# Queries and keys of attention groups 2 and 3 by seven products of quarters

## The chip, the cores and the metric

The kernel runs on one core of a Trainium2 chip. The metric is the device time of one execution in microseconds (us); the time before is the median of three runs. The engines are TensorE (PE in the profile; PEld are its weight loads), VectorE (DVE), ScalarE (ACT), GpSimd (POOL) and SyncE (SP, which issues most DMAs). Each engine works through its own instructions in a fixed order, and semaphores make one engine wait for another.

## The reference

Two layers over 512 tokens of 1024 features, all in float32. Each layer is a token mixer and a gated feed-forward part, both with RMS norms, and shifts, scales and gates made from a condition vector `c` (`ada_w`). Layer 1 mixes with a recurrent mixer (HGRN2), layer 2 with dilated attention. What the change touches is the start of the attention:

```python
proj = (u @ w_in).reshape(B, S, N_GROUPS, 3, ATT_HEADS, ATT_HEAD_DIM)   # 3 groups, 8 heads of 128
for gi, (window, dilation) in enumerate(((128, 1), (512, 4), (2048, 16))):
    q = apply_partial_rope(proj[:, :, gi, 0], cos, sin) * scale
    k = apply_partial_rope(proj[:, :, gi, 1], cos, sin)
    v = proj[:, :, gi, 2]
    o_g, lse_g = dilated_group_attention(q, k, v, window, dilation)
# softmax over the groups' lse weighs the o_g; then o @ w_out
```

So queries are u (512 x 1024) times a 1024 x 128 matrix for each head and group, and keys likewise. With its transpose, one head and group gives a 256 x 1024 weight matrix (128 rows for queries, 128 for keys) times a 1024 x 512 matrix of inputs.

## The kernel before, in words

Every product in float32 precision is made of three matmuls on rounded operands: a value is cut into a rounded part `hi` and a remainder `lo` (ACT copies, then DVE subtracts), and `three` (L437 to L440) adds hi x hi, hi x lo and lo x hi into a PSUM bank. `block` (L442) does this for eight tiles of 128 input features: 24 matmuls with a 128 x 128 weight and 512 tokens.

Weights come through `Stream` (L38). It holds a list of items in the order of use; `fill` loads them into two `raw` buffers of 128 x 2048, `process_to` cuts an item into one of three `hi` and three `lo` buffers (L88 on ACT, L89 on DVE). Between attention weights, items of `ada_w` for the condition vector are woven in; they occupy `raw` buffers too, and DVE multiplies and adds them up (L257, L259), after which POOL reduces over partitions (L261).

The feed-forward parts already use Strassen's scheme in Winograd's form with seven products of quarters instead of eight (`seven_products`, L771 on, products at L853): the inputs' quarters and four sums of them (`th`, `tl`) are made once per layer by `token_sums` (L753), and for each weight block POOL (L824) and DVE (L828, L832) make the sums of weight quarters, and ACT copies partial sums from one PSUM bank into half of another (L883, L892), onto which PE goes on accumulating. There the order of instructions of all engines is written out by hand. Items of the kind "quarters" are four DMAs that lay a weight block out by its four quarters (L56 to L59). The values of groups 2 and 3 are made by seven products as well (`seven_values`, L1383).

In attention the inputs are permuted so that tokens of one residue modulo 4 lie together (`apart`, L1674, with remainders in `apart[1]`). The sums of the quarters of `apart` lie in `uh` and `ul` as `th`, `tl` (L1679 to L1681). The loop at L1852 goes over the units: for head `i` and group `g`, `st.take()` gives the weights (with two items processed ahead), `block` makes queries and then keys, and `qk_evac` (L1694) writes them from PSUM to SBUF on ACT (L1704 the 32 rotary rows, L1705 all rows). `turn_pair` (L1709) applies the rotation on DVE and copies it back on ACT. After each of the six blocks of a head `fl.tick()` runs what is due: scores (L1724), merges, transposes (L1807) and the products with the values of an earlier head. The units of head 1 in groups 1 and 2 come before the first values, then group 3 of head 1 and heads 2 to 5, then the second half of the values, then heads 6 to 8. In this part a scheduler orders each engine's instructions when the kernel is built, by its own estimates of time; it is not written out by hand.

Of the kernel before, what the change touches and what calls it, by code (L numbers as in the profile page):

```python
# [9 lines left out]
F32 = mybir.dt.float32  # L10
# [5 lines left out]
P = 128  # L16
# [21 lines left out]
class Stream:  # L38
# [73 lines left out]
    def whole(self):  # L112

        assert self.items[self.done][0] in WHOLE
        self.fill()
        self.done += 1
        return self.raw.pop(self.done - 1)
# [41 lines left out]
def block_kernel(tc, x, c, positions, ada_w, ada_b, norm_g, hgrn_w_in, lower, hgrn_norm_g, hgrn_w_out,  # L159
# [8 lines left out]
    with ExitStack() as ctx:  # L168
# [215 lines left out]

        def aqk(g, hd):
            return ("w", tuple(AW[:, (g * 3 + k) * D + hd * P:(g * 3 + k) * D + (hd + 1) * P].rearrange(
                "(k p) n -> p k n", p=P) for k in range(2)))
# [49 lines left out]
        def three(ps, ah, al, bh, bl, start, stop):  # L437
            pe.matmul(ps, ah, bh, start=start, stop=False)  # L438
            pe.matmul(ps, ah, bl, start=False, stop=False)  # L439
            pe.matmul(ps, al, bh, start=False, stop=stop)  # L440
# [942 lines left out]
        def seven_values(dsts, apart, th, tl):  # L1383
# [45 lines left out]
            def run(ps, i, tile, o, us):  # L1429
                hi, lo = tiles[i, tile]  # L1430
                for n in range(2):
                    for kt in range(4):
                        w = slice(o * 1024 + kt * 256, o * 1024 + (kt + 1) * 256)
                        three(ps[:, n * 256:(n + 1) * 256], *us(kt, n), hi[:, w], lo[:, w], kt == 0, kt == 3)
# [415 lines left out]

        fl.n = 0
        for kind, g, i in order:  # L1852
            if kind == "v":
                if g == 1:

                    for fn in fl.at.pop(fl.n, []):
                        fn()
                    seven_values(V[1:], apart, th, tl)
                    if i:
                        act.dma_start(V[0], v_away)  # L1860
                continue
            if g == 0:
                heads[i] = {}
                n = fl.n
                fl.add(n + 3, lambda i=i: scores(i, 0))
                fl.add(n + 5, lambda i=i: scores(i, 1))
                fl.add(n + 7, lambda i=i: scores(i, 2))
                fl.add(n + 9, lambda i=i: (merge_r(i), merge_n(i)))
                fl.add(n + 10, lambda i=i: flips_r(i))
                fl.add(n + 11, lambda i=i: pv_r(i))  # L1870
                fl.add(n + 11, lambda i=i: flips_n(i))
                fl.add(n + 12, lambda i=i: pv_n(i))
            whi, wlo = st.take()
            pair = []
            for k in range(2):
                ps = block(whi, wlo, k * D, P, u=apart)
                heads[i]["qk"[k], g] = qk_evac(ps, g, k, pair)
                if k == 1:
                    turn_pair(g, pair)
# [39 lines left out]
```

## Time and profile before

| | |
|---|---|
| median of 3 runs | 1510.74 us (1510.27 to 1512.08) |
| the profiled execution | 1511.44 us, its span 1509.4 us |
| granted TensorE clock, mean | 0.997 |
| DMA | 199.14 MB, mean 132 GB/s |
| ACT busy | 746.6 us (49%) |
| POOL busy | 199.0 us (13%) |

The span is the time from the first to the last instruction of the profiled execution. Busy time is the time in which an engine had at least one instruction under way. Rows that group instructions give the line, the engine, the operation, output and inputs, shapes and number, then the sum of their durations in us and the mean in ns, then the idle time before them and what ended it. In rows by time the first two columns are start and duration in us. A window row gives the stretch and its length, then the busy time and number of instructions of each engine, and at its end the granted clock, the DMA share and GB/s.

### The profile page before, as it was taken

How to read it: one execution, taken by the hardware profiler on the slowest of the kernel's cores; microseconds unless marked ns; L12 is line 12 of the kernel's file. 1: busy time of each engine (PE TensorE's matmuls, PEld its weight loads, DVE VectorE, ACT ScalarE, POOL GpSimd, SP SyncE). 2: the span in 40 equal slices, each digit the busy share in tenths (PEclk: the TensorE clock that was granted, in tenths of full speed). 3: DMA queues.
4: the chain of work that ended last, by engine and by line, in shares of the span. 5: the costliest groups of instructions: out<-in, count | busy, mean ns of one | idle time of the engine just before them, and what ended most of it. 6: DMA issues, size and time to landing. Idle time of an engine off the chain costs nothing. (4 is left out here: it accounts for less than half of the span.)

```text
span 1509.4 us, 23492 instructions
## 1 busy us (share of the span) xinstructions
PE 1493.7 (99%) x9231; PEld 1309.7 (87%) x9231; DVE 1040.2 (69%) x1807; ACT 746.6 (49%) x1321; POOL 199.0 (13%) x174
## 2 busy tenths in 40 slices
PE   8999999999999999999999999999999999999998
PEld 6777888898999988888988888988888899999886
DVE  4587768486888876577668766686466978887533
ACT  4443433362555542376546666356655555555231
POOL 1011211030111101040001110011002211110100
PEclk9999999999999999999999999999999999999999
DMA  9553444125333356424166540365213333334531
GB/s 309 166 183 126 156 152 168 56 85 167 101 109 107 107 200 213 155 108 141 57 183 191 151 120 29 123 185 141 84 52 117 100 97 112 112 112 141 199 108 56
DMA packets 206942, 199.14 MB, mean 132 GB/s; under 512 B 6840, under 2 KB 164720, under 8 KB 206576
## 3 DMA queue, kind: packets, MB, share of 16 engines
q1 hardware_dynamic: 203856, 190.87, 40.3%
q10 hardware_dynamic: 1952, 6.65, 1.2%
q8 instruction: 72, 1.18, 0.3%
q0 software_dynamic: 1024, 0.13, 0.2%
q14 instruction: 38, 0.31, 0.1%
HBM read 192.31 MB, written 5.31 MB: 131 GB/s over the span
## 5 line engine op out<-in xcount | busy, mean ns | idle before, releaser
L88 ACT CAST hi<-raw 128x2048 fp32r<-128x2048 f32 x68 | 129.7, 1907 | 199.1 <-DMA raw<-in_ffn_w_out_dram 60.8
L89 DVE TENSOR_TENSOR lo<-raw,hi 128x2048 fp32r<-128x2048 f32 x68 | 161.5, 2377 | 96.2 <-ACT hi L88 96.2
L438 PE MATMUL ps_mm<-apart,hi 128*128 128x512 f32 x384 | 151.4, 394 | 0.0
L439 PE MATMUL ps_mm<-apart,hi 128*128 128x512 f32 x384 | 151.2, 394 | 0.0
L440 PE MATMUL ps_mm<-apart,lo 128*128 128x512 f32 x384 | 150.6, 393 | 0.0
L438 PE MATMUL ps_mm<-uh,hi 128*128 128x512 f32 (+1 forms) x400 | 146.3, 366 | 0.0
L439 PE MATMUL ps_mm<-ul,hi 128*128 128x512 f32 (+1 forms) x400 | 144.3, 361 | 1.0 <-DVE ul L538 1.0
L440 PE MATMUL ps_mm<-uh,lo 128*128 128x512 f32 (+1 forms) x400 | 144.6, 361 | 0.0
L438 PE MATMUL ps_mm<-hi,oh 128*128 128x512 f32 x240 | 94.0, 392 | 0.0
L853 PE MATMUL ps_mm<-th,hiq 128*128 128x256 f32 x340 | 93.9, 276 | 0.0
L853 PE MATMUL ps_mm<-tl,hiq 128*128 128x256 f32 x340 | 93.9, 276 | 0.0
L853 PE MATMUL ps_mm<-th,loq 128*128 128x256 f32 x340 | 93.9, 276 | 0.0
L439 PE MATMUL ps_mm<-lo,oh 128*128 128x512 f32 x240 | 93.4, 389 | 0.0
L438 PEld LDWEIGHTS ps_mm<-uh,hi 128*128 128x128 f32 x400 | 75.5, 189 | 19.7 <-issue 8.4
L844 DVE TENSOR_TENSOR loq<-raw,hiq 128x1024 fp32r<-128x1024 f32 x68 | 80.2, 1221 | 16.8 <-ACT hiq L840 16.8
L439 PEld LDWEIGHTS ps_mm<-ul,hi 128*128 128x128 f32 x400 | 75.6, 189 | 12.1 <-DVE ul L538 1.4
L440 PEld LDWEIGHTS ps_mm<-uh,lo 128*128 128x128 f32 x400 | 75.5, 189 | 11.4
L824 POOL TENSOR_TENSOR raw<-raw 128x512 f32<-128x512 f32 x34 | 45.1, 1328 | 305.1 <-DVE spare L820 131.3
L440 PEld LDWEIGHTS ps_mm<-apart,lo 128*128 128x128 f32 x384 | 72.2, 188 | 14.5
L439 PEld LDWEIGHTS ps_mm<-apart,hi 128*128 128x128 f32 x384 | 72.2, 188 | 14.2
L438 PEld LDWEIGHTS ps_mm<-apart,hi 128*128 128x128 f32 x384 | 72.2, 188 | 14.1
L259 DVE SCALAR_TENSOR_TENSOR shared<-raw,cond,shared 128x512 f32<-128x512 f32 x98 | 73.2, 747 | 12.9 <-DMA raw<-in_ada_w_dram 11.9
(440 smaller groups left out, 4183.5 us busy)
## 6 DMA issues: line engine op xcount, KB each, us to landing
raw<-in_ada_w_dram SPq DMA_DIRECT2D x40, 1024.0 KB, 5.1
raw<-in_ffn_w_in_dram SPq DMA_DIRECT2D x136, 256.0 KB, 3.6
raw<-in_attn_w_in_dram SPq DMA_DIRECT2D x48, 512.0 KB, 5.1
raw<-in_ffn_w_out_dram SPq DMA_DIRECT2D x22, 1024.0 KB, 4.9
raw<-in_hgrn_w_in_dram SPq DMA_DIRECT2D x12, 1024.0 KB, 5.4
raw<-in_attn_w_in_dram SPq DMA_DIRECT2D x12, 1024.0 KB, 4.9
raw<-in_ffn_w_in_dram SPq DMA_DIRECT2D x10, 1024.0 KB, 5.0
first<-in_ada_w_dram SPq DMA_DIRECT2D x14, 512.0 KB, 7.9
```

The lines of the kernel that those rows point to most:

```text
L88: self.nc.scalar.copy(hi, t)
L89: self.nc.vector.tensor_sub(lo, t, hi.bitcast(F32))
L259: dve.scalar_tensor_tensor(a, r[:, k], sc, a, op0=OP.mult, op1=OP.add)
L438: pe.matmul(ps, ah, bh, start=start, stop=False)
L439: pe.matmul(ps, ah, bl, start=False, stop=False)
L440: pe.matmul(ps, al, bh, start=False, stop=stop)
L824: pool.tensor_add(r[:, 2], r[:, 2], r[:, 0])
L844: dve.tensor_sub(lo, src, hi.bitcast(F32))
L853: pe.matmul(ps, w[x][:, a], us[kt][y], start=begin and kt + m == 0, stop=kt == 3 and m == 2, skip_group_check=True)
```

## The change

For groups 2 and 3 (`g > 0`) of all eight heads, the items of the stream become "quarters": the four quarters of the 256 x 1024 weight matrix, of 128 x 512 each, with keys first. `sevens` makes a unit out of seven products of quarters, each of 4 x 3 matmuls with 256 tokens. `prepare_1` makes three of the seven weight operands in a first pair of hi/lo buffers: quarter 1 (its remainder on POOL), the sum of quarters 1 and 0, and that sum plus quarter 2. Quarter 0 gets quarter 2 added on POOL. `prepare_2` cuts all four places of the altered `raw` into a second pair. `products_1` makes three products, and copies partial sums on ACT from `first` to `u2` and from `u2` to `u4`; `products_2` adds the other four onto them. The queries come straight out of two banks, on ACT, with their sign turned. The keys are two sums on DVE of an SBUF copy (`xs`) and a PSUM bank. Each unit takes half of each of the four "mm" banks. Group 1 keeps its two blocks. `queries_keys` prepares up to two steps ahead of the products (a unit by seven is two steps). `three` passes `skip_group_check` on to the matmuls, and in `seven_values` only the first matmul of a bank has the start flag, where each half had it. `whole` first processes what stands ahead of it in the stream. The scheduler orders this part as before.

```diff
--- before.py
+++ after.py
@@ -111,7 +111,7 @@
 
     def whole(self):
 
-        assert self.items[self.done][0] in WHOLE
+        self.process_to(next(i for i in range(self.done, len(self.items)) if self.items[i][0] in WHOLE))
         self.fill()
         self.done += 1
         return self.raw.pop(self.done - 1)
@@ -382,9 +382,11 @@
         def av(g, hf):
             return [wtok(AW, kq, (g * 3 + 2) * D + hf * 512) for kq in range(2)]
 
+        by_seven = lambda g: g > 0
+
         def aqk(g, hd):
-            return ("w", tuple(AW[:, (g * 3 + k) * D + hd * P:(g * 3 + k) * D + (hd + 1) * P].rearrange(
-                "(k p) n -> p k n", p=P) for k in range(2)))
+            w = [AW[:, (g * 3 + k) * D + hd * P:(g * 3 + k) * D + (hd + 1) * P].rearrange("(k p) n -> p k n", p=P) for k in range(2)]
+            return ("quarters", (w[1], w[0])) if by_seven(g) else ("w", tuple(w))
 
         order, at = [], []
 
@@ -434,10 +436,10 @@
             act.copy(hi, src)
             dve.tensor_sub(lo, src, hi.bitcast(F32))
 
-        def three(ps, ah, al, bh, bl, start, stop):
-            pe.matmul(ps, ah, bh, start=start, stop=False)
-            pe.matmul(ps, ah, bl, start=False, stop=False)
-            pe.matmul(ps, al, bh, start=False, stop=stop)
+        def three(ps, ah, al, bh, bl, start, stop, part=False):
+            pe.matmul(ps, ah, bh, start=start, stop=False, skip_group_check=part)
+            pe.matmul(ps, ah, bl, start=False, stop=False, skip_group_check=part)
+            pe.matmul(ps, al, bh, start=False, stop=stop, skip_group_check=part)
 
         def block(whi, wlo, c0, width, ps=None, tok=slice(0, S), kts=range(KT), u=(uh, ul)):
 
@@ -1431,7 +1433,7 @@
                 for n in range(2):
                     for kt in range(4):
                         w = slice(o * 1024 + kt * 256, o * 1024 + (kt + 1) * 256)
-                        three(ps[:, n * 256:(n + 1) * 256], *us(kt, n), hi[:, w], lo[:, w], kt == 0, kt == 3)
+                        three(ps[:, n * 256:(n + 1) * 256], *us(kt, n), hi[:, w], lo[:, w], kt + n == 0, kt == 3, True)
 
             H2 = lambda a: a.rearrange("p (n c) -> p n c", n=2)
             for step in range(3):
@@ -1848,36 +1850,143 @@
                     pe.matmul(b[:, sl], V[0][:, t - 1, hs], st_["p0"][:, sl], start=False, stop=True)
             dve.tensor_add(oT[hd], oT[hd], b)
 
+        def sevens(g, hd):
+
+
+            raw, hi_lo = [], [None, None]
+            Q = lambda t, k, n=1: t[:, k * 512:(k + n) * 512]
+            a_of = lambda r, c: [[a[:, r * 4 + k, c * 256:c * 256 + 256] for a in apart] for k in range(4)]
+            t_of = lambda i: [[a[:, i, k] for a in (th, tl)] for k in range(4)]
+            t1, T3, T4, t2 = (t_of(i) for i in range(4))
+
+            def cut(part, k, sub):
+                hi, lo = hi_lo[0]
+                act.copy(Q(hi, part), Q(raw[0], k))
+                sub.tensor_sub(Q(lo, part), Q(raw[0], k), Q(hi, part).bitcast(F32))
+
+            def add(to, k, eng):
+                eng.tensor_add(Q(raw[0], to), Q(raw[0], to), Q(raw[0], k))
+
+            def prepare_1():
+                raw.append(st.whole())
+                hi_lo[0] = st.part_tiles(R0)
+                cut(0, 1, pool)
+                add(1, 0, dve)
+                cut(1, 1, dve)
+                add(0, 2, pool)
+                add(1, 2, dve)
+                cut(2, 1, dve)
+                add(1, 3, dve)
+
+            def prepare_2():
+                hi, lo = hi_lo[1] = st.part_tiles(R0)
+                t = raw.pop()
+                act.copy(hi, t)
+                dve.tensor_sub(lo, t, hi.bitcast(F32))
+                st.fill()
+
+            def run(ps, half, part, us, begin):
+                hi, lo = hi_lo[half]
+                for kt in range(4):
+                    w = slice(part * 512 + kt * P, part * 512 + (kt + 1) * P)
+                    three(ps, hi[:, w], lo[:, w], *us[kt], begin and kt == 0, kt == 3, True)
+
+            def products_1():
+                first, both, u2, u4 = banks = [bank("mm")[:, 0:256] for _ in range(4)]
+                xs = fresh(mk, [P, 512], "xs", 1)
+                run(first, 0, 0, a_of(0, 0), True)
+                act.copy(u2, first)
+                run(both, 0, 1, T3, True)
+                act.copy(xs[:, 0:256], both)
+                run(u2, 0, 2, t2, False)
+                act.copy(u4, u2)
+                return banks, xs
+
+            def products_2(banks, xs):
+                first, both, u2, u4 = banks
+                flip_no[1] += 1
+                o = flip_no[1] % 2 * 256
+                rows = shared[:, 1, o:o + 256]
+                q, k = (fresh(mk, [P, S], "qk", 6) for _ in range(2))
+                heads[hd]["q", g], heads[hd]["k", g] = q, k
+                lo, hi = slice(0, 256), slice(256, 512)
+                run(first, 1, 3, a_of(1, 0), False)
+                act.activation(rows[0:32], first[0:32], AF.Copy, scale=-SCALE)
+                act.activation(q[:, lo], first, AF.Copy, scale=-SCALE)
+                run(u4, 1, 0, t1, False)
+                act.copy(xs[:, 256:512], u4)
+                run(u2, 1, 2, T4, False)
+                dve.tensor_add(k[:, hi], xs[:, 256:512], both)
+                dve.tensor_add(k[:, lo], xs[:, 0:256], u2)
+                act.copy(rows[96:P], k[0:32, hi])
+                act.copy(rows[64:96], k[0:32, lo])
+                run(u4, 1, 1, a_of(1, 1), False)
+                act.activation(rows[32:64], u4[0:32], AF.Copy, scale=-SCALE)
+                act.activation(q[:, hi], u4, AF.Copy, scale=-SCALE)
+                turn_pair(g, [rows, q, k])
+            got = []
+            return [(prepare_1, lambda: got.extend(products_1())), (prepare_2, lambda: products_2(*got))]
+
+        def plain(g, hd):
+            got = []
+
+            def prepare():
+                got.extend(st.take(0))
+
+            def products():
+                pair = []
+                for k in range(2):
+                    ps = block(*got, k * D, P, u=apart)
+                    heads[hd]["qk"[k], g] = qk_evac(ps, g, k, pair)
+                    if k == 1:
+                        turn_pair(g, pair)
+                    fl.tick()
+            return [(prepare, products)]
+
+        def begin_head(i):
+            heads[i] = {}
+            n = fl.n
+            fl.add(n + 3, lambda: scores(i, 0))
+            fl.add(n + 5, lambda: scores(i, 1))
+            fl.add(n + 7, lambda: scores(i, 2))
+            fl.add(n + 9, lambda: (merge_r(i), merge_n(i)))
+            fl.add(n + 10, lambda: flips_r(i))
+            fl.add(n + 11, lambda: pv_r(i))
+            fl.add(n + 11, lambda: flips_n(i))
+            fl.add(n + 12, lambda: pv_n(i))
+
+        def queries_keys(units):
+
+            steps = []
+            for g, hd in units:
+                two = sevens(g, hd) if by_seven(g) else plain(g, hd)
+                steps += [(g, hd, k, *p) for k, p in enumerate(two)]
+            ahead = 0
+            for n, (g, hd, k, prepare, products) in enumerate(steps):
+                while ahead < min(len(steps), n + 3):
+                    steps[ahead][3]()
+                    ahead += 1
+                if (g, k) == (0, 0):
+                    begin_head(hd)
+                products()
+                if by_seven(g):
+                    fl.tick()
+
         fl.n = 0
+        units = []
         for kind, g, i in order:
-            if kind == "v":
-                if g == 1:
-
-                    for fn in fl.at.pop(fl.n, []):
-                        fn()
-                    seven_values(V[1:], apart, th, tl)
-                    if i:
-                        act.dma_start(V[0], v_away)
-                continue
-            if g == 0:
-                heads[i] = {}
-                n = fl.n
-                fl.add(n + 3, lambda i=i: scores(i, 0))
-                fl.add(n + 5, lambda i=i: scores(i, 1))
-                fl.add(n + 7, lambda i=i: scores(i, 2))
-                fl.add(n + 9, lambda i=i: (merge_r(i), merge_n(i)))
-                fl.add(n + 10, lambda i=i: flips_r(i))
-                fl.add(n + 11, lambda i=i: pv_r(i))
-                fl.add(n + 11, lambda i=i: flips_n(i))
-                fl.add(n + 12, lambda i=i: pv_n(i))
-            whi, wlo = st.take()
-            pair = []
-            for k in range(2):
-                ps = block(whi, wlo, k * D, P, u=apart)
-                heads[i]["qk"[k], g] = qk_evac(ps, g, k, pair)
-                if k == 1:
-                    turn_pair(g, pair)
-                fl.tick()
+            if kind == "qk":
+                units.append((g, i))
+            elif g == 1:
+                queries_keys(units)
+                units = []
+
+                for fn in fl.at.pop(fl.n, []):
+                    fn()
+                seven_values(V[1:], apart, th, tl)
+                if i:
+                    act.dma_start(V[0], v_away)
+        queries_keys(units)
         fl.at.clear()
         upx.close()
         tail = {-1: [lambda: pv_n(6), lambda: scores(7, 2), mkx.close], 2: [lambda: merge_r(7), back(0)], 3: [lambda: merge_n(7)],
```

## The prediction

> **What bounds the kernel now.** I read the page's engine rows first, then busy time by stage, then what PE waits for.
>
> ```profile
> PE 1493.7 (99%) x9231; PEld 1309.7 (87%) x9231; DVE 1040.2 (69%) x1807; ACT 746.6 (49%) x1321; POOL 199.0 (13%) x174
> ```
> ```profile
> 400.00:500.00 100.00, 100.00 (x878) 100.00 (x877) 80.44 (x83) 58.46 (x95) 12.93 (x10) 1.00 0.38 108
> 740.00:760.00 20.00, 20.00 (x171) 20.00 (x170) 16.12 (x20) 7.84 (x8) 0.58 (x1) 1.00 0.17 54
> 780.00:944.00 164.00, 163.63 (x834) 138.05 (x833) 114.56 (x339) 104.43 (x221) 24.16 (x20) 1.00 0.44 129
> 992.00:1120.00 128.00, 127.84 (x659) 108.68 (x658) 76.99 (x253) 82.74 (x177) 15.23 (x16) 1.00 0.40 116
> ```
> ```profile
> PE ps_b L1837 <- ACT h L1815: 0.3, 1, 0.3
> ```
>
> After the length of a stage, each window row gives PE, PEld, DVE, ACT and POOL with their counts, then the granted clock, DMA share and rate. The rows are the seven products of the first feed-forward part (400 to 500), those of the values (740 to 760), and the two stretches that make queries and keys: 780 to 944 (group 3 of head 1, heads 2 to 5) and 992 to 1120 (heads 6 to 8). In both PE does not stop; the last row is its whole list of waits from 775 to 945, 0.3 us. So these stretches last as long as PE's work, and matmul time taken out of them is won while no other engine becomes late. DVE is next: 114.6 of 164 us (70%) in the first, 77.0 of 128 (60%) in the second. The first has more because the products of the condition vector with its weights are woven into it.
>
> **PE's part.** A unit (queries and keys of one head and group) is 48 matmuls 512 wide; by seven products it is 7 x 12 = 84 matmuls 256 wide. Durations of matmuls overlap, so I count starts.
>
> ```profile
> 804.76 0.39 PE L439 MATMUL ps_mm<-apart,hi 128*128 128x512 f32 x1
> ...
> 815.19 0.39 PE L440 MATMUL ps_mm<-apart,lo 128*128 128x512 f32 x1
> ```
>
> The second is the 46th after the first: 10.43 / 46 = 0.2267 us each, 48 x 0.2267 = 10.88 us a unit. For 256 columns, the values' window has 171 in 20 us, 0.1170 each, a unit 9.82; the feed-forward window has 878 in 100 us, 0.1139 each, a unit 9.57. A unit saves 1.06 or 1.31 us, the sixteen units of groups 2 and 3 save 16.9 or 21.0. I take 16.9, since the values read the same tiles (apart, and the sums in uh and ul) through the same helper; 21.0 stays as a bound. The small matmuls of the scores are untouched.
>
> [...]
>
> **What is added for it.** Rows for the same operations elsewhere (mean ns of one after the comma):
>
> ```profile
> L832 DVE TENSOR_TENSOR raw<-raw 128x512 f32<-128x512 f32 x34 | 23.5, 691 | 1.1
> L435 DVE TENSOR_TENSOR ol<-mid,oh 128x512 fp32r<-128x512 f32 x44 | 29.8, 686 | 25.8 <-ACT oh L434 25.7
> L860 DVE TENSOR_TENSOR shared<-shared,ps_a 128x256 f32<-128x256 f32 x17 | 7.0, 413 | 0.0
> L824 POOL TENSOR_TENSOR raw<-raw 128x512 f32<-128x512 f32 x34 | 45.1, 1328 | 305.1 <-DVE spare L820 131.3 <-DVE loq L820 119.4 <-DMA raw<-in_ffn_w_in_dram 54.4
> L538 POOL TENSOR_TENSOR ul<-u,uh 128x512 fp32r<-128x512 f32 x20 | 30.4, 1545 | 7.4 <-ACT uh L534 7.4
> L434 ACT CAST oh<-mid 128x512 fp32r<-128x512 f32 x44 | 26.2, 619 | 62.3 <-PE ps_b L439 47.7 <-PE ps_mm L439 10.4 <-DVE shared L259 1.4
> L892 ACT COPY ps_mm<-ps_mm 128x256 f32<-128x256 f32 x34 | 12.1, 357 | 33.6 <-PE ps_mm L853 33.6
> L904 ACT COPY shared<-ps_mm 128x256 f32<-128x256 f32 x34 | 12.7, 372 | 4.8 <-PE ps_mm L853 4.7
> L905 ACT ACTIVATE shared<-ps_b 128x256 f32<-128x256 f32 x17 | 6.6, 390 | 0.0
> L1705 ACT ACTIVATE qk<-ps_mm 128x512 f32<-128x512 f32 x48 | 28.8, 599 | 0.9
> ```
> ```profile
> 811.30 0.68 DVE L306 TENSOR_TENSOR gate<-shared,raw 128x512 f32<-128x512 f32 x1
> 811.91 0.15 DVE L1791 TENSOR_TENSOR wE<-wE,wZ 128x4 f32<-128x4 f32 x1
> ```
>
> DVE gets, per unit, three sums and two remainders of 512 and two key sums of 256 out of PSUM: 5 x 0.69 + 2 x 0.41 = 4.27 us. The two rows in order of time show the next instruction starting 0.61 us into a 0.68 us one; the windows count that overlap once, so with 0.07 off each it is 3.8 us. ACT gets three copies of 512 (1.86), four of PSUM (2 x 0.357 + 2 x 0.372 = 1.46) and two query halves (0.78), and loses two evacuations (1.20): 2.9 us. POOL gets one remainder and one sum, 1.5 + 1.3. The 2048-wide copy and remainder stay. The 32-row copies are as many as before. DMA brings the same bytes in four pieces.
>
> ACT in the first stretch: 104.4 + 9 x 2.9 = 130.5 of about 154 us, 85%, and it is not the limit. **DVE is.** Nine units by seven lie in this stretch, six in the second, one (head 1, group 2) before the first values. First stretch: PE 164 - 9 x 1.06 = 154.5; DVE 114.6 + 9 x 3.8 = 148.8, 96%. Second: PE 128 - 6.4 = 121.6; DVE 77.0 + 22.8 = 99.8, 82%, about the 80% at which the feed-forward window runs without a stop.
>
> There is one more charge. In time order, POOL's sum and a DVE instruction with two SBUF inputs, then the same DVE instruction with POOL quiet:
>
> ```profile
> 433.84 1.29 POOL L824 TENSOR_TENSOR raw<-raw 128x512 f32<-128x512 f32 x1 [8.31 <-DVE spare L820]
> ...
> 434.47 1.21 DVE L862 SCALAR_TENSOR_TENSOR mid<-shared 128x512 f32<-128x512 f32 x1
> ```
> ```profile
> 531.94 0.68 DVE L862 SCALAR_TENSOR_TENSOR mid<-shared 128x512 f32<-128x512 f32 x1
> ```
>
> DVE, started 0.63 us after POOL, lost 0.53 us. An overlapped POOL instruction can thus cost DVE from 0 (DVE waiting for it, or working out of PSUM) to its 1.3 us. I take 0.53, as in this row: 18 such in the first stretch, 9.5 us, and 12 in the second, 6.4.
>
> So in the first stretch DVE needs 148.8 + 9.5 = 158.3 us, more than PE's 154.5. It also waits in order for ACT's copies and for scores. I put that at 3 us of those of its 49 idle us that cannot be filled (bounds 0, and 12, a quarter): 161.3 us, 2.7 saved instead of 9.5. A plain unit's weights go through one copy and one remainder, 4.3 us:
>
> ```profile
> L88 ACT CAST hi<-raw 128x2048 fp32r<-128x2048 f32 x68 | 129.7, 1907 | 199.1 <-DMA raw<-in_ffn_w_out_dram 60.8 <-PE ps_mm L439 40.0 <-DMA raw<-in_attn_w_in_dram 31.9
> L89 DVE TENSOR_TENSOR lo<-raw,hi 128x2048 fp32r<-128x2048 f32 x68 | 161.5, 2377 | 96.2 <-ACT hi L88 96.2
> ```
>
> The new chain is ACT, POOL, DVE, ACT, DVE, DVE, ACT, DVE, DVE, ACT, DVE: 3 x 0.62 + 1.55 + 5 x 0.69 + 1.91 + 2.38 = 11.2 us, and a unit now takes two of the three hi/lo buffers. Its first half can begin when the unit before the last is done, one unit (9.8 us) ahead of its use, and needs 6.2 of them. So DVE cannot work far ahead, and behind a late remainder of DVE stand PE's next product, in order, and POOL's and ACT's next steps.
>
> In the second stretch DVE has 106.2 us of 121.6; PE's gain of 6.4 holds less 1.5 where the stretch begins. Unit 2 of head 1 gains 1.1; it holds one of two raw buffers longer, and already before, the values' second half waited for its load:
>
> ```profile
> 714.66 2.00 ACT L1395 CAST hiq<-raw 128x1024 fp32r<-128x1024 f32 x2 [3.29 <-DMA raw<-in_attn_w_in_dram]
> ```
>
> I take 1.5 us lost there (bounds 0 and the chain's 11.2 - 4.3 = 6.9 us). Sum: 2.7 + 4.9 - 0.4 = 7.2 us; I take 6.5 for the profiled run of 1511.44 us (span 1509.4), which is 0.05% above the median 1510.74: **1505 us**.
>
> **Rivals.** (a) *All of it is won*: POOL's steps fall where DVE waits anyway, and the scheduler hides the rest. For it: DVE below 100% without the charge; at 80% the feed-forward part has no stop. Against: 96%. 1511.4 - 16.9 to 21.0 = 1490 to 1495, with up to 5 us of stalls 1499.
>
> (b) *POOL holds DVE up fully, slower*: each of POOL's steps costs 1.3 us. [...] The rows of L862 agree with it in kind: its end, 435.68, is POOL's end, 435.13, and 0.55 more. First stretch: 148.8 + 18 x 1.3 + 3 = 175.2 against 164, 11 lost; second: 99.8 + 15.6 = 115.4 of 121.6, some 3 kept. About 1519. With x for a step, the first stretch changes by 148.8 + 18x + 3 - 164 and the rest wins 4.5: slower than before from x = 0.93 us.
>
> (c) *DVE gives back just the gain*: with the waits at 12 us the first stretch is 170.3, 6 lost, the others win 4.5 and less; 1511 to 1513. That the products don't get shorter is excluded by the values' window.
>
> **How the numbers follow.** The forecast, 1501 to 1508.5: 0.40. (a) 1490 to 1500: 0.17. (b) 1514 to 1525: 0.28. (c) 1508.5 to 1514: 0.15. The range 1496 to 1520 leaves out about half of (a) and a quarter of (b). A change below 0.2% (3 us) cannot be told from none here. Faster by more (under 1507.7): (a) and most of the forecast, 0.51. Slower by more (over 1513.8): (b) and a little of (c), 0.30. Within: 0.19.
>
> **What would show it.** Right: matmuls 256 wide at 0.114 to 0.118 us from start to start; in the first stretch DVE at 95% or more and PE waiting on DVE's remainders or merges for some 6 to 8 us, hardly any in the second; L1865 and L1868 on POOL at 1.3 us, and DVE instructions beside them lengthened. Wrong: PE with no waits (a); PE waiting 15 us or more (b); waits of PE mainly on ACT's copies into PSUM, or on loads, which I priced at nothing.

## The result, and the profile after

Median 1581.31 us of 4 runs (1579.72 to 1583.48) against 1511.41 of 4 runs of the kernel before (1510.27 to 1516.11): ratio 1.0457, 95% interval 1.0432 to 1.0483. The change makes the kernel slower by 70 us; the forecast was 1505, with a range up to 1520. The profiled execution has a span of 1579.1 us.

The page's engine row of the changed kernel, and busy time by stage: the stretch that makes queries and keys behind the first values, the second half of the values, and the stretch of queries and keys behind these. In the changed kernel's numbering the lines of this part are two higher than before.

```profile
PE 1501.7 (95%) x9807; PEld 1341.2 (85%) x9807; DVE 1117.8 (71%) x1919; ACT 788.2 (50%) x1433; POOL 251.2 (16%) x206
```
```profile
768.60:981.00 212.40, 177.48 (x1192) 164.32 (x1191) 152.82 (x400) 126.98 (x281) 51.01 (x37) 0.91 0.38 110
981.00:1026.40 45.40, 44.88 (x381) 44.71 (x380) 37.81 (x71) 21.38 (x34) 1.04 (x2) 1.00 0.36 117
1026.40:1162.00 135.60, 120.63 (x832) 111.75 (x832) 100.36 (x260) 85.58 (x189) 32.73 (x25) 0.96 0.35 102
```

The same three stretches of the kernel before:

```profile
769.00:941.00 172.00, 171.63 (x859) 144.33 (x859) 121.16 (x348) 104.85 (x221) 23.61 (x19) 1.00 0.47 135
941.00:987.00 46.00, 46.00 (x391) 45.92 (x391) 29.10 (x42) 17.59 (x22) 0.55 (x1) 1.00 0.35 115
987.00:1106.00 119.00, 118.84 (x598) 100.55 (x597) 73.29 (x241) 74.02 (x157) 14.49 (x14) 1.00 0.46 134
```

The values take as long as before; the two other stretches are 40 and 17 us longer. PE, which stood for 0.5 us in these two, now stands for 34.9 + 15.0 us, and its granted clock is 0.91 and 0.96 where it was 1.00. DVE is busy for 152.8 of 212.4 us (72%) and 100.4 of 135.6 (74%): no engine is full. What PE waits for from 676 to 1163 us (sum, times, longest):

```profile
PE ps_a L1745 <- ACT qk L1722: 20.3, 5, 7.8
PE ps_mm L440 <- ACT ps_mm L1902: 9.2, 3, 4.7
PE ps_mm L440 <- ACT ps_mm L1898: 6.5, 2, 3.4
PE ps_mm L442 <- DVE lo L89: 5.0, 1, 5.0
PE ps_mm L442 <- DVE loq L1885: 3.6, 3, 1.6
```

Scores wait for ACT's copies into q and k, products for ACT's copies from PSUM to PSUM, and least of all for DVE's remainders. One such stop, by the rows of four engines in order of time:

```profile
795.00 3.25 POOL L261 PARTITION_ALL_REDUCE shared<-shared  x1 [7.16 <-DVE shared L259]
805.45 1.25 POOL L1865 TENSOR_TENSOR loq<-raw,hiq 128x512 fp32r<-128x512 f32 x1 [7.20 <-issue]
...
806.74 0.69 DVE L1868 TENSOR_TENSOR raw<-raw 128x512 f32<-128x512 f32 x1 [3.12 <-POOL loq L1865]
807.46 0.62 ACT L1864 CAST hiq<-raw 128x512 fp32r<-128x512 f32 x1 [5.07 <-DVE raw L1868]
...
807.74 1.49 DVE L1717 TENSOR_TENSOR shared<-shared,rot 128x256 f32<-128x256 f32 x1
809.32 2.63 ACT L1722 COPY qk<-shared 32x256 f32<-32x256 f32 x4 [0.96 <-DVE sR L1771]
...
812.00 1.22 PE L1745 MATMUL ps_a<-qk,qk 128*128 128x128 f32 x3 [6.21 <-ACT qk L1722]
```

POOL ends its reduction at 798.25 and starts the unit's remainder 7.20 us later, held by nothing that the profile shows. DVE's sum waits for that remainder, ACT's next copy for the sum. The head's rotation (L1717) and ACT's copies into q and k stand behind these in the queues, although they need none of it, and PE behind them. After a stop PE is slow:

```profile
854.50 3.36 PE L1745 MATMUL ps_a<-qk,qk 128*128 128x128 f32 x8 [4.66 <-ACT qk L1722]
...
858.08 0.41 PE L442 MATMUL ps_mm<-uh,loq 128*128 128x256 f32 x1
858.30 0.41 PE L440 MATMUL ps_mm<-uh,hiq 128*128 128x256 f32 x1
...
859.85 0.28 PE L440 MATMUL ps_mm<-apart,hiq 128*128 128x256 f32 x1
859.96 0.28 PE L441 MATMUL ps_mm<-apart,hiq 128*128 128x256 f32 x1
```
```profile
854.00:858.00 4.00, 3.50 (x10) 2.96 (x11) 0.00 (x0) 0.71 (x2) 0.00 (x0) 0.50 0.00 1
```

For some 5 us after a stop of 4.66 us the spacing is 0.21 us in place of 0.11, at a granted clock of 0.50.

Stage by stage: attention runs from the first cast of `apart` to the first cast of `oT`; from there to the second feed-forward part's first product with `th` lies the output product with what follows. Kernel before, then after:

```profile
L1676 ACT CAST apart<-uh x8: 1106/1126/1142, 676.4 to 683.6; 128x512 fp32r<-128x512 f32 x8
L434 ACT CAST oh<-oT x6: 604/615/622, 1106.5 to 1118.3; 128x512 fp32r<-128x512 f32 x6
L853 PE MATMUL ps_mm<-th,hiq x90: 276/276/281, 1212.7 to 1299.7; 128*128 128x256 f32 x90
```
```profile
L1678 ACT CAST apart<-uh x8: 1106/1124/1137, 675.3 to 682.5; 128x512 fp32r<-128x512 f32 x8
L436 ACT CAST oh<-oT x6: 605/616/621, 1162.3 to 1180.6; 128x512 fp32r<-128x512 f32 x6
L855 PE MATMUL ps_mm<-th,hiq x20: 276/276/281, 1282.7 to 1297.7; 128*128 128x256 f32 x20
```

Attention takes 487.0 us in place of 430.1, and the stage behind it 120.4 in place of 106.2: +56.9 and +14.2, with the rest as it was. I added up the starts of PE's rows in attention. 768 matmuls at 0.2276 us gave way to 1344 at 0.1170, 17.6 us won. The waits that the rows list ahead of PE's instructions sum to 51.9 us (23 stops), against 1.1 before: 50.8 lost. The rest of the 56.9, some 24 us, is wider spacing. Most of that comes with the clock: it is granted at 0.50 in nine stretches of attention, 47.8 us in all, 10.9 of them within stops, so half of the other 36.9, some 18 us, is lost (an estimate from the 0.21 us in place of 0.11 above). The 14.2 of the next stage:

```profile
1165.83 0.50 PE L440 MATMUL ps_mm<-hi,oh 128*128 128x512 f32 x1 [3.32 <-ACT hi L88]
1168.74 0.79 PE L441 MATMUL ps_mm<-lo,oh 128*128 128x512 f32 x1 [2.41 <-DVE lo L89]
1188.12 0.79 PE L440 MATMUL ps_mm<-hi,oh 128*128 128x512 f32 x1 [3.79 <-ACT hi L88]
```

PE waits there for its weights to be split, four times and for 11.1 us in all, which never happened at this place before.

### The profile page after: what moved, and what is told of

The parts are those of the page before. It is cut to its first block, busy times and chain, and to the rows that moved or that the text cites. A ratio compares the mean times of both kernels' runs of the same rounds, so it can differ in the third digit from the quotient of the medians.

```text
span 1579.1 us, 25064 instructions
## 1 busy us (share of the span) xinstructions
PE 1501.7 (95%) x9807; PEld 1341.2 (85%) x9807; DVE 1117.8 (71%) x1919; ACT 788.2 (50%) x1433; POOL 251.2 (16%) x206
## 3 DMA queue, kind: packets, MB, share of 16 engines
q0 software_dynamic: 1024, 0.13, 0.2%
## 5 line engine op out<-in xcount | busy, mean ns | idle before, releaser
L88 ACT CAST hi<-raw 128x2048 fp32r<-128x2048 f32 x52 | 99.1, 1906 | 146.8 <-DMA raw<-in_ffn_w_out_dram 64.7
L89 DVE TENSOR_TENSOR lo<-raw,hi 128x2048 fp32r<-128x2048 f32 x52 | 123.4, 2374 | 63.9 <-ACT hi L88 63.9
L440 PE MATMUL ps_mm<-uh,hiq 128*128 128x256 f32 x256 | 78.7, 308 | 17.2 <-ACT ps_mm L1902 9.2
L261 POOL PARTITION_ALL_REDUCE shared<-shared x14 | 50.3, 3590 | 206.5 <-DVE shared L259 197.5
L842 ACT CAST hiq<-raw 128x1024 fp32r<-128x1024 f32 x68 | 68.1, 1048 | 17.6 <-DVE raw L830 16.8
L442 PE MATMUL ps_mm<-uh,loq 128*128 128x256 f32 x256 | 75.1, 295 | 0.9 <-DVE loq L1865 0.9
L441 PE MATMUL ps_mm<-ul,hiq 128*128 128x256 f32 x256 | 75.3, 294 | 0.0
L1864 ACT CAST hiq<-raw 128x512 fp32r<-128x512 f32 x48 | 29.7, 619 | 85.2 <-DVE raw L1868 58.0
```

What stands on the lines that cost most here:

```text
L88: self.nc.scalar.copy(hi, t)
L89: self.nc.vector.tensor_sub(lo, t, hi.bitcast(F32))
L261: pool.partition_all_reduce(a, a, P, bass.bass_isa.ReduceOp.add)
L440: pe.matmul(ps, ah, bh, start=start, stop=False, skip_group_check=part)
L441: pe.matmul(ps, ah, bl, start=False, stop=False, skip_group_check=part)
L442: pe.matmul(ps, al, bh, start=False, stop=stop, skip_group_check=part)
```

## The experiments

The theory after this reading, called S: PE stops because POOL, DVE and ACT do a unit's steps in order, and a step that starts late holds all that is queued behind it; POOL's late start after a reduction, and the output weights that are no longer split ahead, are the two places where it is plainest. Rival D: DVE, and what POOL's steps beside it cost it, as the prediction had it. Where nothing else is said, the time is that of one run. Single runs of the kernel before, beside them, took 1510.75 to 1514.03 us, and three runs of e12_half 1539.92 to 1547.04, so a difference under some 4 us is not read, and one of 4 to 9 us is weak evidence unless the trace bears it out. The table has the stages as above, attention (A) and what follows up to the second feed-forward part (O).

| kernel | us | A | O |
|---|---|---|---|
| before | 1511.44 | 430.1 | 106.2 |
| after | 1581.19 | 487.0 | 120.4 |
| e1_no_reduce | 1562.39 | 468.1 | 120.9 |
| e2_dve | 1560.03 | 463.9 | 121.0 |
| e3_group3 | 1588.82 | 494.3 | 120.0 |
| e4_no_sums | 1533.52 | 437.4 | 120.6 |
| e5_seam | 1575.04 | 492.4 | 107.8 |
| e6_aside | 1556.98 | 463.8 | 119.5 |
| e7_no_seed | 1524.80 | 428.0 | 121.8 |
| e8_dve_seam | 1544.65 | 466.0 | 106.0 |
| e9_two_tiles | 1543.87 | 448.2 | 120.1 |
| e10_amount | 1555.04 | 460.3 | 120.3 |
| e11_later | 1538.26 | 457.4 | 106.2 |
| e12_half | 1541.98 | 462.5 | 106.4 |
| e13_all_plain | 1512.93 | 431.9 | 106.2 |
| e14_spread | 1543.55 | 463.5 | 106.3 |
| e15_half_no_sums | 1513.21 | 434.2 | 106.4 |
| e16_half_tiles | 1522.73 | 444.6 | 105.5 |
| e17_half_amount | 1540.31 | 459.9 | 108.0 |

### POOL: reductions left out, steps given to DVE, half the units

In e1_no_reduce the reductions over partitions that lie in attention are not made:

```diff
-                if kq == 1:
+                if kq == 1 and not (l == 1 and v in (2, 3, 4)):
```

e2_dve gives POOL's two steps to DVE, and e3_group3 makes only group 3 by seven products:

```diff
-                cut(0, 1, pool)
+                cut(0, 1, dve)
...
-                add(0, 2, pool)
+                add(0, 2, dve)
```
```diff
-        by_seven = lambda g: g > 0
+        by_seven = lambda g: g > 1
```

> The changed kernel without the six partition reductions on POOL (L261) in attention; the layer's shift, scale and gate are then not summed over partitions. Theory S (after a reduction POOL's next tensor instruction, the remainder L1865, starts only 7 to 9 us later, and DVE, ACT and PE stand in order behind it): six times 6 to 8 us of PE's stop go, 1533 to 1550. Rival D (DVE has too much work and the chain of eleven steps is too long for three buffers): the reductions hold DVE up 2 us each at most, 1568 to 1580.

> The changed kernel with both POOL steps of a unit (the remainder of quarter 1 and the sum of quarters 0 and 2) given to DVE. Theory S: no tensor instruction is left behind a reduction, DVE gets 16 x 1.2 = 20 us more: 1520 to 1550. Rival D: DVE is already the limit, 20 us more on it make it slower: 1590 to 1605.

> Seven products for group 3 only, eight units; group 2 is made as before. Theory S: PE's gain and the number of remainders behind a reduction both halve: the 70 us become about 35, 1540 to 1555. Rival D: DVE in the first stretch falls from 96% to about 83% and the chain has a plain unit ahead of it to hide in: 1500 to 1515.

Measured: 1562.39, 1560.03 and 1588.82. Without the reductions 19 us go, more than D allowed and less than S. The waits that POOL's late start made are nearly gone; the changed kernel first, then e1_no_reduce.

```profile
POOL loq L1865 <- issue: 23.1, 3, 8.9
DVE raw L1868 <- POOL loq L1865: 22.1, 6, 7.3
```
```profile
DVE raw L1868 <- POOL loq L1865: 1.2, 1, 1.2
```

With POOL's steps on DVE 21 us go, although DVE has more to do: this speaks against D, by which it would have become slower; S had expected more of it, 1520 to 1550. The 21 us are what the two steps cost by being on POOL at all, their late starts and what they do to DVE beside them (below) together. But 49 us remain. e3_group3 failed both theories: eight units fewer and 7.5 us slower. One of its two longest stops (12.2 and 11.8 us) shows POOL's late start whole, here in front of the flips of a head (L1812):

```profile
805.72 3.25 POOL L261 PARTITION_ALL_REDUCE shared<-shared  x1 [8.42 <-DVE shared L1717]
816.17 1.25 POOL L1868 TENSOR_TENSOR raw<-raw 128x512 f32<-128x512 f32 x1 [7.19 <-issue]
```
```profile
817.45 1.90 ACT L1884 CAST hiq<-raw 128x2048 fp32r<-128x2048 f32 x1 [9.58 <-POOL raw L1868]
```
```profile
825.33 0.90 PE L1812 MATMUL ps_a<-ident,h 128*128 128x128 f32 x3 [11.77 <-DVE sN L1750]
```

Halving the units did not halve the late starts: behind five of its six reductions POOL's next tensor instruction still starts 7.1 to 7.5 us late. So this run does not price a start; it shows that PE can stop for 12 us when a head's work stands behind one.

### The output product's weights split ahead

```diff
+                if last and n >= len(steps) - 2:
+                    st.process_to(st.wpos[st.taken + n - len(steps) + 2] + 1)
                 products()
```

with `last` true for the last stretch: e5_seam from the changed kernel, e8_dve_seam from e2_dve.

> The changed kernel, whole, with one thing put back: ahead of the last unit's two halves one weight item each is split for the output product that follows, as the kernel before has them ready. Theory S (the stretch from the first split of attention's output to the second feed-forward, 120.4 us against 106.2, is longer only because its weights are split just in time): 1565 to 1568, and that stretch at 106 to 108. Rival (the stretch is longer because attention's tail, its last scores and merges, now lies in it): 1576 to 1580, and the stretch at 118 or more.

> The changed kernel with POOL's two steps of each unit on DVE (as e2_dve, 1560.0) and the output product's weights split ahead (as e5_seam), computing all of it. If the two losses are separate: 1545 to 1549. Rival (the time won at the seam is lost again, since ACT and DVE have the splits in front of the last unit's copies): 1553 to 1560.

Measured: 1575.04, with O at 107.8, and 1544.65, with O at 106.0. The stage is back at its old length in both, so the 14.2 us came from the weights being split just in time: `st.take()` prepared two items ahead, and the last unit thereby split the next product's weights; the changed kernel prepares inside a list of units that ends with the last unit. The time of e5_seam lies outside both expectations, since only 6 of the 14 us arrive: A is 5.4 us longer, a little more than single runs differ by, and why stays open. In e8_dve_seam the gain arrives whole (15.4).

### Sums and splits: their row, their amount, their tiles

e4_no_sums splits a unit's weights once, as for a plain unit, into one pair of tiles, and makes no sums:

```diff
             def prepare_1():
                 raw.append(st.whole())
-                hi_lo[0] = st.part_tiles(R0)
-                cut(0, 1, pool)
...
-                add(1, 3, dve)
...
-                hi, lo = hi_lo[1] = st.part_tiles(R0)
+                hi_lo[0] = hi_lo[1] = st.part_tiles(R0)
```

e6_aside (from e2_dve) keeps three splits and four sums, but the sums come last:

```diff
-                cut(0, 1, dve)
-                add(1, 0, dve)
...
+                for part in range(3):
+                    cut(part, 1, dve)
...
                 dve.tensor_sub(lo, t, hi.bitcast(F32))
+                for to, k in ((1, 0), (0, 2), (1, 2), (1, 3)):
+                    add(to, k, dve)
```

e9_two_tiles (from e4_no_sums) has the one split in two halves in two pairs of tiles; e10_amount has one pair and three more splits and four sums, unused:

```diff
+            def halves(k):
+                hi, lo = hi_lo[k] = st.part_tiles(R0)
+                act.copy(Q(hi, 2 * k, 2), Q(raw[0], 2 * k, 2))
+                dve.tensor_sub(Q(lo, 2 * k, 2), Q(raw[0], 2 * k, 2), Q(hi, 2 * k, 2).bitcast(F32))
```
```diff
+                hi_lo[0] = hi_lo[1] = st.part_tiles(R0)
+                for part in range(3):
+                    cut(part, part, dve)
...
+                for to, k in ((1, 0), (0, 2), (1, 2), (1, 3)):
+                    add(to, k, dve)
```

> The changed kernel with the weights of a unit prepared as for a plain one (one copy and one remainder of 2048, no sums of quarters; all seven products read this one pair of buffers, so their values are not the reference's). What is left of the change is the 84 matmuls, the copies into PSUM and the sums of keys. Theories S and D both: PE's gain alone, 16 x 1.06 to 1.35, 1489 to 1496. A rival that blames ACT's copies into half banks or the order of the products: PE still stops at them, 1520 or more.

> The kernel of e2_dve (1560.0; no work of the units on POOL) with the same instructions in another order: the three quarters of the first half are split as they came, and the four sums are made behind the split of the second half, where nothing waits for them. What it leaves out: the products then use quarters that were not summed. DVE and ACT have the same amount of work as in e2_dve, but no split waits for a sum. Theory C (chain: the in-order run of sum, ACT's copy, DVE's difference delays the copies out of PSUM and the scores): 1530 to 1545, near e4_no_sums (1533.5). Theory A (amount: DVE has too much to do): 1554 to 1565.

> The kernel of e4_no_sums (1533.5; four quarters of a unit split once, into one of the three pairs of tiles) with the same amount of splitting in two pairs of tiles, two quarters in each, as a changed unit takes two pairs. What it leaves out, as e4_no_sums: the products use quarters that were not summed. Theory T (tiles: with two of three pairs taken per unit, ACT's next split waits for PE to leave a pair, and all behind it on ACT waits too; this is what separates e2_dve, 1560.0, from e4_no_sums): 1545 to 1560. Theory A (amount of work on ACT and DVE): 1530 to 1537.

> The kernel of e4_no_sums with the amount of work of e2_dve and still one pair of tiles for a unit: three quarters are split a second time into the same places, and four sums are made that nobody uses. Theory A (amount): 1552 to 1565, as e2_dve. Theory T (tiles): 1533 to 1540. Between these: both have a part, in proportion.

Measured: 1533.52, 1556.98, 1543.87 and 1555.04. S and D both missed e4_no_sums, for which they expected 1489 to 1496: without splits and sums the change still costs 22 us, 14 of them in O. The chain of sums is not what costs: with the sums where nothing waits for them, e6_aside is 3 us under e2_dve, and not at 1530 to 1545. In A, e4_no_sums has 437.4; two pairs of tiles add 10.8, the amount alone adds 22.9, both as they are (e2_dve) 26.5. So it is mostly the amount, and in part the tiles. But the amount does not fill DVE: here are e2_dve and e4_no_sums.

```profile
680.00:1130.00 450.00, 416.45 (x2903) 388.48 (x2902) 357.83 (x833) 276.72 (x561) 41.35 (x35) 0.97 0.38 113
```
```profile
680.00:1115.00 435.00, 416.88 (x2998) 391.20 (x2997) 296.21 (x750) 256.83 (x530) 39.74 (x36) 0.99 0.41 120
```

DVE is at 80% in the one and 68% in the other. So the work does not lack room on DVE. That it costs by standing ahead of work for which PE waits is my reading of stops like the one above.

### Copies into PSUM, and the place of the scores

e7_no_seed is e4_no_sums without the copies by which a half bank begins as another; e11_later is e8_dve_seam with a head's first scores one step later:

```diff
-                act.copy(u2, first)
-                act.copy(u4, u2)
```
```diff
-            fl.add(n + 3, lambda: scores(i, 0))
+            fl.add(n + 4, lambda: scores(i, 0))
```

> The kernel of e4_no_sums (1533.5) without the two copies of 128x256 by which a half bank begins as a copy of another; the products that were accumulated onto the copy begin their bank instead. What it leaves out: the first product is missing from three of the four quarters of the result. Theory P (PE's queue stops at the products behind these copies, since the copies stand behind other work of ACT): attention 20 to 25 us shorter than in e4_no_sums, 1508 to 1515. Rival (what e4_no_sums still loses is at the scores and in the pitch, not at the copies): 1526 to 1533.

> The kernel of e8_dve_seam (1544.65, all of it computed) with each head's first scores (line 1745) one step later. PE stood 18.8 us before these, for ACT's last copies into q and k, and a changed step is shorter than the one it replaced. If it is this distance: the stops at the scores go, and some of the slow clock behind them: 1520 to 1532. Rival (ACT and DVE are late anyway, and the stop only moves to the copies into PSUM or the next split): 1540 to 1550.

Measured: 1524.80 and 1538.26. The copies cost 8.7 us, less than half of what I expected; with them and the sums gone, A is 428.0 against 430.1 before: 11.6 us of stops and some 5 us of wider spacing still use up nearly all of the 17.6 us of shorter matmuls. In e11_later the stops before the scores fell from 18.8 to 1.8 us, but copies into PSUM took their place. First e8_dve_seam, then e11_later:

```profile
PE ps_a L1745 <- ACT qk L1722: 18.8, 8, 5.3
PE ps_mm L440 <- ACT ps_mm L1898: 5.6, 4, 2.9
```
```profile
PE ps_mm L440 <- ACT ps_mm L1898: 8.3, 5, 3.3
PE ps_mm L440 <- ACT ps_mm L1902: 7.1, 4, 3.0
...
PE ps_a L1745 <- ACT qk L1722: 1.8, 2, 1.0
```

The time lies between the two expectations, 6.4 us under e8_dve_seam: a large part of a stop that is moved away comes back at the next place.

### Half the units, without POOL and with the seam closed

e12_half is e8_dve_seam with `by_seven = lambda g: g > 1`, e13_all_plain the same with `g > 2`, so with no unit by seven.

> The kernel of e8_dve_seam (1544.65: no work on POOL, the output product's weights split ahead, all of it computed) with seven products only for the eight units of group 3. Half of PE's gain, about 8.8 us, and half of the added splits and sums. If what the stops cost grows with the number of units: half way to the kernel before, about 1528. If ACT and DVE keep up with half of the added work (it grows faster than their load): 1505 to 1518, and stops of PE in attention under 12 us against 45 in e8_dve_seam. If it is rather the shape of a changed unit (two steps, copies into PSUM) whatever the load: 1528 to 1540.

> The kernel of e12_half with no unit by seven products: every unit of queries and keys as in the kernel before, in the changed kernel's control flow (all units of a stretch in one list, two steps prepared ahead), and the output product's weights split ahead. All of it is computed. If the changed units make the loss: the time of the kernel before, 1508 to 1516. Rival (the new control flow moves the order on the engines and costs by itself): 1525 or more.

e12_half: 1541.98 in the profiled run, 1539.92 and 1547.04 in two others, against a median of 1512.91 of 7 runs of the kernel before, ratio 1.0197 (1.0160 to 1.0234; a fourth execution, of 2728.06 us, is left out). e13_all_plain: 1512.93. So the new control flow costs nothing that a single run shows, and half of the units costs as much as all: 29 us over the kernel before, with sixteen units 31. That is nearest to the third case of the expectation, the shape of a unit whatever the load. Four kernels look for the reason. e14_spread makes the first half's splits and sums in two portions, the second behind a plain unit's first product; e15_half_no_sums, e16_half_tiles and e17_half_amount are e4_no_sums, e9_two_tiles and e10_amount with eight units and the output product's weights split ahead.

```diff
                 cut(1, 1, dve)
+                mid.append(prepare_1b)
+
+            def prepare_1b():
                 add(0, 2, dve)
...
                     fl.tick()
+                    flush()
```

> The kernel of e12_half (1541.98) with the first half's three splits and four sums made in two portions, the second behind the first product of the plain unit beside them; the amount is the same, all of it is computed. Theory B (burst: some 5 us of a changed unit's work come on DVE in a row, and a head's merge, its masks and its flips stand behind them, once per head): the stops of PE before the flips (line 1812, 14.6 us) go, 1515 to 1530. Rival (it is not the row but the sum of the work, or its place): 1538 to 1546.

> The kernel of e12_half with one split of the weights per changed unit, as a plain unit has, and no sums. What it leaves out: the seven products use quarters that were not summed. If the added splits and sums make the loss: 1505 to 1515. Rival (the seven products with their copies into PSUM, the loads and the control flow make it): 1525 to 1540.

> The kernel of e15_half_no_sums (1513.21; eight units by seven products, four quarters split once, into one pair of tiles) with the same splits in two pairs of tiles, two quarters in each. What it leaves out: the products use quarters that were not summed. Theory T (tiles: fewer pairs left for splitting ahead): 1530 to 1545. Theory A (amount): 1511 to 1518. Both, as with sixteen units (there +10.3 for the tiles, +21.5 for the amount): 1520 to 1526.

> The kernel of e15_half_no_sums with the amount of work of e12_half and still one pair of tiles for a unit: three quarters split a second time into the same places, and four sums that nobody uses. Theory A (amount): 1532 to 1545. Theory T (tiles): 1511 to 1518. Both, in proportion to sixteen units: 1524 to 1536.

Measured: 1543.55, 1513.21, 1522.73 and 1540.31. The splits and sums make 28.3 us of A (434.2 to 462.5); in one row or in two is the same. Their amount alone makes 25.7, a second pair of tiles alone 10.4: the answer of the sixteen units, and nearly the same numbers. The third case goes with this: e15_half_no_sums keeps the shape of a unit, its two steps and its copies into PSUM, and costs nothing. PE's longest waits in e12_half:

```profile
PE ps_a L1812 <- DVE sN L1750: 14.6, 7, 3.0
PE ps_mm L440 <- ACT ps_mm L1898: 3.3, 2, 2.8
```

The flips (L1812) of four of the eight heads wait for DVE, 2.9 to 5.4 us each, and with sixteen units the scores wait once per head (e8_dve_seam, 18.8 us in 8 stops). That would fit a price per head more than one per unit, but it is not shown: no kernel here changed the number of waits alone. Why eight units' work delays a head as much as sixteen's stays open. A version with these stages later was not tried on the chip; the last head's remaining stages are placed by hand, and they would have had to change too. Nor was another order of the same instructions tried, beyond e6_aside, e11_later and e14_spread: the scheduler chooses it by its own estimates, and how much of the loss is its order stays open.

No kernel that computes all of it with any unit by seven came below e11_later, 1538.26. Even those without sums did not win: e15_half_no_sums is 1513.21, and e7_no_seed with 15 us off for the seam would be at about 1510 (an estimate from its O of 121.8 and e8_dve_seam's 106.0).

## Why the prediction was wrong

- **Matmuls: right.** The mean of all spacings of 256 columns under 0.16 us in attention after 745 us is 0.1167 us; 17.6 us were won, where 16.9 was taken.
- **Durations: right.** In the three stretches, with fifteen units by seven, DVE's busy time rose from 223.6 to 291.0 us, 67.4; of that, 15.6 is lengthening beside POOL (below), and 51.8 the work, 3.5 us a unit (forecast 3.8). POOL's two steps have medians of 1.29 and 1.41 us.
- **"I put that at 3 us": the step that failed.** The first stretch was to last as long as DVE's work with its charge, 158.3 us, and 3 us (bound 12) of DVE's idle time that cannot be filled, as if an engine that is not full kept all others supplied. None of it was filled: DVE's idle time was 50.8 of 172 us before and is 59.6 of 212.4 now, so DVE came to 72%, not to 96%, because the stretch grew. What set its length were PE's stops, 34.9 us in the first stretch and 15.0 in the second, and the slow clock behind them, which the sum did not have. The trace of before showed DVE at 70% with no stop; it did not show that an order in which all waits fit stays so when 3 to 4 us per unit are put ahead of a head's rotation, copies and merges. That a late remainder of DVE holds up PE, POOL and ACT stood in the prediction, but without a price.
- **POOL's start: priced at nothing.** POOL was counted with its durations. That a tensor instruction behind a reduction started 6.9 to 8.9 us after its end is nowhere in the sum; e1_no_reduce puts it at 19 us, and e2_dve, which takes the lengthening of DVE away too, at 21.
- **The charge on DVE for POOL's steps beside it: right in size.** From 765 us on, 16 of DVE's instructions took longer beside one of POOL's 30 steps than the median of their line, 7.5 us in the first stretch and 8.1 in the second, 15.6 in all (forecast 9.5 + 6.4), 0.52 us a step. Each of them ended with POOL's step or up to 0.55 us behind it, however small it was:

```profile
1116.57 1.43 POOL L1865 TENSOR_TENSOR loq<-raw,hiq 128x512 fp32r<-128x512 f32 x1 [4.10 <-ACT hiq L1864]
1116.77 1.25 DVE L1791 TENSOR_TENSOR wZ<-wZ 128x4 f32<-128x4 f32 x1
```

Line 1717 had two such of 23, at 1.49 and 1.50 us; after, and e2_dve, where none is lengthened so:

```profile
L1717 DVE TENSOR_TENSOR shared<-shared,rot x23: 406/420/1497, 718.1 to 1153.7; 128x256 f32<-128x256 f32 x23
```
```profile
L1717 DVE TENSOR_TENSOR shared<-shared,rot x23: 409/418/427, 719.3 to 1132.3; 128x256 f32<-128x256 f32 x23
```

What this is worth by itself was not isolated: e1_no_reduce keeps it, and e2_dve takes it away together with the late starts and gives DVE the two steps.
- **"PE's gain of 6.4 holds less 1.5 where the stretch begins": failed** for the same reason, 15.0 us of stops at a DVE of 74%. That 80% in the feed-forward part was no measure, since its order is written out by hand and this one comes from a scheduler's estimates, is a guess that no run tests.
- **The output product: not seen.** 14.2 us, for a call that took a 0 where it took two ahead. The diff showed it.
- **The clock behind a stop: not priced.** Some 24 us of wider spacing in attention.
- **Copies into PSUM: priced at nothing**, named as what would prove the forecast wrong; 15.7 us of waits in the changed kernel, 8.7 us by e7_no_seed.
- **Rivals.** (b) had the sign, and PE waiting for more than 15 us, but for another reason: each of POOL's steps was to cost DVE its whole 1.3 us, and cost it 0.52. Its 1519 was 62 us short. None had a price for a stop in one engine's queue passed on to all.

The sum of what was isolated, from after to before, in the order in which the kernels remove it: POOL's steps 21 us, the seam 15, the added splits and sums with their tiles 26 (e2_dve to e4_no_sums), copies into PSUM 9: 71 us, against the 70 lost. That these add up is in part assumed, since the kernels of the last two steps do not have the seam closed. What is left after that are the 17.6 us won and about as many of stops and wider spacing.

## What to carry to other kernels

Where one engine is busy at 99% because every other one is just in time, price an edit that adds work to the others by whose work stands behind it in their queues, and not by their free share: with DVE at 72 to 74% and ACT at 60 to 63%, PE stood for 50 us here. Price each stop of PE with its slow restart (1.6 to 3.2 us more behind each of eight stops here), and ask of every engine that is given a new kind of instruction what it did just before. When a loop over items is rebuilt, look also at what its lookahead did for the stage behind it.

## What was not expected of the hardware

In the three places where nothing else held it (23.1 us in all), a tensor instruction on POOL started 7.0 to 8.9 us after the end of a reduction over partitions; behind the three other reductions of attention it was 6.9 to 8.3. There is a row for a change of POOL's configuration at 798.2 us, where the reduction ends:

```profile
L1865 POOLq MODIFY_POOL_CONFIG  x12: 98/98/98, 798.2 to 1091.9; - x12
```

It takes 0.1 us; what fills the rest of the wait no row shows: it is listed as "issue", 7.20 us at 805.45, 7.19 in e3_group3. A start 6.9 to 8.9 us late comes behind each of the six reductions in attention, not once.

The clock: after each of the eight stops of 3 us or more in the changed kernel's attention, PE lost 1.6 to 3.2 us more by wider spacing within the next 7 us. The clock is granted at 0.50 in or just behind these eight stops, for 3.4 or 6.8 us. But shorter stops brought it too: two of 1.48 and 0.90 us, 0.5 us apart (0.50 for 10.2 us from 774.0 on), and one of 2.86 us in e12_half (up to 818.05; the spacing behind it is 0.21 us from 820.03 to 824.08), while behind one of 2.77 us in e12_half (up to 1037.48) the clock stayed at 1.00.
